# Adjusting contrast on one core: from phases of loads and stores on one DMA queue to half-size tiles on two queues

## The chip, the core and the metric

The kernel runs on one core of a Trainium2 chip. TensorE multiplies matrices, VectorE (DVE in the profile) and ScalarE (ACT) work on tiles in the on-chip memory SBUF, GpSimd (POOL) prepares constants, and SyncE (SP) issues DMA transfers. The data moves between the chip's HBM and SBUF through 16 DMA engines that belong to the core. The metric is the device time of the whole kernel in microseconds; lower is better.

## The reference

The input is 48 planes (16 images of 3 channels) of 512 x 512 float32. Every plane is pushed away from its own mean by a factor of 1.5 and clipped.

```python
def reference(x, factor):            # x: (16, 3, 512, 512) float32, factor 1.5
    mean = np.mean(x, axis=(2, 3), keepdims=True)
    return np.clip(mean + factor * (x - mean), 0, 1).astype(np.float32)
```

A plane has 1 MiB, so 50.33 MB are read and 50.33 MB are written. No pixel can be written before the whole plane has been read.

## The kernel before

The input is taken as one long row of numbers. A tile is 128 partitions with `ROW` = 16384 numbers (64 KB) each, 8 MiB in all, and contiguous in HBM; sixteen partitions hold one plane (`ppi`), a tile eight planes. There are six tiles, and a ring in SBUF with three slots (`BUFS` = 3); tile `t` lies in slot `t % BUFS` from its load to its store and is changed in place.

The steps of a tile, in `compute`:

- `add` sums each partition's row. VectorE reduces the first `SUM` = 4352 columns (line 85), ScalarE copies the rest onto itself with an accumulator (line 89). Tile 0 is summed in two halves, since it is loaded in pieces.
- TensorE (line 100) multiplies the sums with `blockw`, a matrix that is (1 − factor) / pixels within each block of sixteen partitions and zero elsewhere. The result, `shift`, is in every partition what must be added after the multiplication by the factor.
- VectorE runs over the row twice: multiply by the factor and add `shift` (line 103), then maximum with 0 and minimum with 1 (line 106).
- `store` (line 80) sends the row out. Tile 0 leaves in two pieces, cut at column `SHORT` = 2048.

The work is written out by hand in the order in which each engine does it: five loads for tiles 0 to 2, the computing and storing of tiles 0 to 2, the loads of tiles 3 to 5 (line 77), the computing and storing of tiles 3 to 5. Loads and stores are all issued by SyncE, so they stand in a single DMA queue in that order: three tiles in, three out, three in, three out. A load into a slot waits until the store that emptied it has finished. Synchronisation between the engines is derived from which tiles they read and write.

Of the kernel before, what the change touches and what calls it, by code (L numbers as in the profile page):

```python
# [1 line left out]

# [4 lines left out]


P = 128  # L10
ROW = 16384
HALF = ROW // 2
BUFS = 3
SHORT = 2048
SUM = 4352


@with_exitstack
def kernel(
    ctx: ExitStack,  # L20
    tc: tile.TileContext,
    x: bass.AP,
    factor: float,
    out: bass.AP,
):

    nc = tc.nc
    f32 = mybir.dt.float32  # L30
    Alu = mybir.AluOpType
    Act = mybir.ActivationFunctionType

    B, C, H, W = x.shape
    n_img, n_pix = B * C, H * W
    ppi = n_pix // ROW
    per_tile = P // ppi
    n_tiles = n_img // per_tile
    assert ppi * ROW == n_pix and per_tile * n_tiles == n_img

    factor = float(factor)
    wconst = (1.0 - factor) / float(n_pix)

    x_f = x.rearrange("b c h w -> (b c h w)")
    out_f = out.rearrange("b c h w -> (b c h w)")

    def dram(ap, t, c0=0, c1=ROW):
        return bass.AP(tensor=ap.tensor, offset=t * P * ROW + c0, ap=[[ROW, P], [1, c1 - c0]])

    consts = ctx.enter_context(tc.tile_pool(name="consts", bufs=1))  # L50
    xpool = ctx.enter_context(tc.tile_pool(name="xpool", bufs=1))
    small = ctx.enter_context(tc.tile_pool(name="small", bufs=1))
    psum = ctx.enter_context(tc.tile_pool(name="psum", bufs=1, space=bass.MemoryType.PSUM))


    sums = small.tile([P, 4 * n_tiles], f32, name="sums")
    bias = psum.tile([P, n_tiles], f32, name="bias")

    blockw = consts.tile([P, P], f32, name="blockw")
    blocks = blockw.rearrange("p (a b) -> p a b", b=ppi)  # L60
    nc.gpsimd.memset(blockw, wconst)  # L61
    for base, step in ((0, -ppi), (ppi - 1, ppi)):
        nc.gpsimd.affine_select(  # L63
            out=blocks,
            in_=blocks,
            compare_op=Alu.is_ge,
            fill=0.0,
            base=base,
            pattern=[[step, per_tile], [0, ppi]],
            channel_multiplier=1 if step < 0 else -1,  # L70
        )


    ring = xpool.tile([P, BUFS, ROW], f32, name="ring")

    def load(t, c0=0, c1=ROW):
        nc.sync.dma_start(out=ring[:, t % BUFS, c0:c1], in_=dram(x_f, t, c0, c1))  # L77

    def store(t, c0=0, c1=ROW):
        nc.sync.dma_start(out=dram(out_f, t, c0, c1), in_=ring[:, t % BUFS, c0:c1])  # L80

    def add(t, col, c0, c1, c2):
        xt = ring[:, t % BUFS, :]
        own = sums[:, 4 * t + col : 4 * t + col + 2]
        nc.vector.tensor_reduce(  # L85
            out=own[:, 0:1], in_=xt[:, c0:c1], axis=mybir.AxisListType.X, op=Alu.add
        )
        part = xt[:, c1:c2]
        nc.scalar.activation(out=part, in_=part, func=Act.Copy, accum_out=own[:, 1:2])  # L89
        return [own[:, 1:2], own[:, 0:1]]  # L90

    def compute(t, *cuts):
        xt = ring[:, t % BUFS, :]
        if t == 0:
            parts = add(t, 0, 0, SUM, HALF) + add(t, 2, HALF, HALF + SUM, ROW)
        else:
            parts = add(t, 0, 0, SUM, ROW)
        shift = bias[:, t : t + 1]
        for k, part in enumerate(parts):
            nc.tensor.matmul(shift, blockw, part, start=k == 0, stop=k == len(parts) - 1)  # L100
        for c0, c1 in zip((0, *cuts), (*cuts, ROW)):
            part = xt[:, c0:c1]
            nc.vector.tensor_scalar(  # L103
                out=part, in0=part, scalar1=factor, scalar2=shift, op0=Alu.mult, op1=Alu.add
            )
            nc.vector.tensor_scalar(  # L106
                out=part, in0=part, scalar1=0.0, scalar2=1.0, op0=Alu.max, op1=Alu.min
            )
            store(t, c0, c1)

    with tc.manual_schedule():
        load(0, 0, SHORT)
        load(0, SHORT, HALF)
        load(0, HALF, ROW)
        load(1)
        load(2)
        compute(0, SHORT)
        compute(1)
        compute(2)
        load(3)  # L120
        load(4)
        load(5)
        compute(3)
        compute(4)
        compute(5)


# [1 line left out]
_INS = ['x', 'factor']  # L129
_OUTS = [((16, 3, 512, 512), 'float32')]  # L130

_NUMBERS = {'factor': 1.5}


# [26 lines left out]
```

## Time and profile before

| | |
|---|---|
| time, median of 3 runs | 239.53 us (239.49 to 239.54) |
| span of the profiled execution | 237.3 us |
| HBM read / written | 50.33 MB / 50.33 MB |
| VectorE busy | 137.4 us (58%) |
| ScalarE busy | 59.9 us (25%) |
| TensorE matmul busy | 7.9 us (3%) |

The profiled execution has no time of its own beside its span; the timed runs lie 2.2 us above the span. In the rows, the first number is the start in microseconds from the span's start, or a busy time; PE is TensorE, SPq is the queue of SyncE's DMA issues; "L89" is line 89 of the kernel; the text behind an arrow "<-" in brackets names what ended the idle time before. In grouped rows, the numbers behind the bar are total busy microseconds, mean nanoseconds of one instruction, and idle time before it.

### The profile page before, as it was taken

How to read it: one execution, taken by the hardware profiler on the slowest of the kernel's cores; microseconds unless marked ns; L12 is line 12 of the kernel's file. 1: busy time of each engine (PE TensorE's matmuls, PEld its weight loads, DVE VectorE, ACT ScalarE, POOL GpSimd, SP SyncE). 2: the span in 40 equal slices, each digit the busy share in tenths (PEclk: the TensorE clock that was granted, in tenths of full speed). 3: DMA queues.
4: the chain of work that ended last, by engine and by line, in shares of the span. 5: the costliest groups of instructions: out<-in, count | busy, mean ns of one | idle time of the engine just before them, and what ended most of it. 6: DMA issues, size and time to landing. Idle time of an engine off the chain costs nothing.

```text
span 237.3 us, 186 instructions
## 1 busy us (share of the span) xinstructions
PE 7.9 (3%) x28; PEld 6.9 (3%) x28; DVE 137.4 (58%) x21; ACT 59.9 (25%) x15; POOL 1.1 (0%) x7
## 2 busy tenths in 40 slices
PE   0010100010001000000000000100000000000000
PEld 0010100010001000000000000100000000000000
DVE  0071899949998998000000043499989998991000
ACT  2051300980492000000000049319509800000000
POOL 1000000000000000000000000000000000000000
DMA  7999989899799798989899998989899998989894
GB/s 289 418 442 442 530 353 530 353 486 398 331 464 454 341 530 353 530 353 519 365 442 442 398 486 353 530 354 530 353 475 409 431 453 376 508 353 530 353 530 177
DMA packets 2160, 100.66 MB, mean 424 GB/s; under 512 B 240, under 2 KB 240, under 8 KB 240
## 3 DMA queue, kind: packets, MB, share of 16 engines
q1 hardware_dynamic: 2160, 100.66, 98.7%
HBM read 50.33 MB, written 50.33 MB: 424 GB/s over the span
## 4 chain that ended last, share of the span: by engine, by line
DVE 43%; DMA 36%; ACT 9%; PE 2%; SPq 1%; issue 0%; DVEq 0%; ACTq 0%
DMA ring<-in_x_dram 36%; DVE ring L103 18%; DVE ring L106 18%; ACT ring L89 9%; DVE sums L85 6%; PE bias L100 2%; SPq L77 1%; SPq L80 0%; DVEq L103 0%; ACTq L89 0%
## 5 line engine op out<-in xcount | busy, mean ns | idle before, releaser
L89 ACT ACTIVATE ring<-ring 128x12032 f32<-128x12032 f32 (+1 forms) x7 | 58.0, 8280 | 128.2 <-DMA ring<-in_x_dram 128.2
L85 DVE TENSOR_REDUCE sums<-ring 128x1 f32<-128x4352 f32 x7 | 32.8, 4683 | 63.9 <-DMA ring<-in_x_dram 63.9
L103 DVE TENSOR_SCALAR ring<-ring,bias 128x16384 f32<-128x16384 f32 (+2 forms) x7 | 52.8, 7538 | 12.9 <-PE bias L100 12.9
L106 DVE TENSOR_SCALAR ring<-ring 128x16384 f32<-128x16384 f32 (+2 forms) x7 | 52.3, 7476 | 0.2
L100 PE MATMUL bias<-sums,blockw 128*128 128x1 f32 x28 | 7.9, 360 | 189.1 <-ACT ring L89 175.4
L100 PEld LDWEIGHTS bias<-sums,blockw 128*128 128x128 f32 x28 | 6.9, 314 | 190.0 <-ACT ring L89 159.4
L89 ACT ACT_TABLE_LOAD x1 | 1.3, 1283 | 0.8 <-PEq L142 0.8
L89 ACT ACTIVATION_READ_ACCUMULATOR ring<-ring 128x1 f32 x7 | 1.3, 187 | 0.0
L63 POOL TENSOR_SCALAR_AFFINE_SELECT blockw<-blockw 128x128 f32<-128x128 f32 x2 | 0.7, 340 | 0.1
L61 POOL MEMSET blockw<- 128x128 f32 x1 | 0.2, 204 | 0.3 <-POOLq L142 0.3
L142 POOL MEMSET const-bfloat16-1.0<- 128x1 bf16 x1 | 0.1, 102 | 0.0
L142 POOL MEMSET const-uint8-127<- 128x1 uint8 x1 | 0.1, 102 | 0.0
L142 POOL MEMSET const-float32-0.0<- 128x1 f32 x1 | 0.1, 98 | 0.3 <-issue 0.3
L142 POOL MEMSET const-float32-1.0<- 128x1 f32 x1 | 0.1, 98 | 0.0
## 6 DMA issues: line engine op xcount, KB each, us to landing
out_dram<-ring SPq DMA_DIRECT2D x1, 7168.0 KB, 35.9
ring<-in_x_dram SPq DMA_DIRECT2D x1, 4096.0 KB, 20.8
ring<-in_x_dram SPq DMA_DIRECT2D x1, 3072.0 KB, 11.6
ring<-in_x_dram SPq DMA_DIRECT2D x1, 1024.0 KB, 4.7
out_dram<-ring SPq DMA_DIRECT2D x1, 1024.0 KB, 34.3
ring<-in_x_dram SPq DMA_DIRECT2D x5, 57.7
out_dram<-ring SPq DMA_DIRECT2D x5, 27.0
```

Of the source, the lines that this page charges most:

```text
L61: nc.gpsimd.memset(blockw, wconst)
L63: nc.gpsimd.affine_select(out=blocks, in_=blocks, compare_op=Alu.is_ge, fill=0.0, base=base, pattern=[[step, per_tile], [0, ppi]], channel ...
L77: nc.sync.dma_start(out=ring[:, t % BUFS, c0:c1], in_=dram(x_f, t, c0, c1))
L85: nc.vector.tensor_reduce(out=own[:, 0:1], in_=xt[:, c0:c1], axis=mybir.AxisListType.X, op=Alu.add)
L89: nc.scalar.activation(out=part, in_=part, func=Act.Copy, accum_out=own[:, 1:2])
L100: nc.tensor.matmul(shift, blockw, part, start=k == 0, stop=k == len(parts) - 1)
L103: nc.vector.tensor_scalar(out=part, in0=part, scalar1=factor, scalar2=shift, op0=Alu.mult, op1=Alu.add)
L106: nc.vector.tensor_scalar(out=part, in0=part, scalar1=0.0, scalar2=1.0, op0=Alu.max, op1=Alu.min)
L142: nc = _bacc.Bacc("TRN2", target_bir_lowering=False, num_devices=1)
```

## The change

Tiles have half the row, 8192 numbers (32 KB, 4 MiB a tile), so there are twelve of them, in a ring of six slots that occupies the same memory. SyncE issues loads alone: tiles 0 and 1 each in one transfer, tiles 2 and 3 in one of 8 MiB, tiles 4 and 5 likewise, and then one tile at a time, each when its slot is free. Stores are issued by ScalarE, on its own DMA queue. The sums of all tiles but the first are made by ScalarE alone; in tile 0 VectorE still reduces 4352 of the 8192 columns. Tile 0 is clipped and stored in three pieces of 1024, 2048 and 5120 columns (4, 8 and 20 KB a row). The order is a software pipeline: while VectorE clips tile `t`, ScalarE sums tile `t + 1`; for tiles 1 and 3 the store is issued ahead of that sum, for the others after it. The load of tile `t + 5` is issued after tile `t` in the program's order, and waits for the store of tile `t − 1`.

```diff
-ROW = 16384
-HALF = ROW // 2
-BUFS = 3
-SHORT = 2048
-SUM = 4352
+ROW = 8192
+BUFS = 6
+FIRST = (1024, 3072)
...
+    def load(t, n=1):
+        nc.sync.dma_start(out=slots(t, n), in_=dram(x_f, t, n=n))
 
     def store(t, c0=0, c1=ROW):
-        nc.sync.dma_start(out=dram(out_f, t, c0, c1), in_=ring[:, t % BUFS, c0:c1])
+        nc.scalar.dma_start(out=dram(out_f, t, c0, c1), in_=slots(t, 1, c0, c1))
...
+    def add(t, c0=0):
+        own = sums[:, 2 * t : 2 * t + 2]
+        parts = []
+        if c0:
+            nc.vector.tensor_reduce(
+                out=own[:, 0:1], in_=slots(t, 1, 0, c0), axis=mybir.AxisListType.X, op=Alu.add
+            )
+            parts.append(own[:, 0:1])
+        part = slots(t, 1, c0)
         nc.scalar.activation(out=part, in_=part, func=Act.Copy, accum_out=own[:, 1:2])
+        parts.insert(0, own[:, 1:2])
         shift = bias[:, t : t + 1]
         for k, part in enumerate(parts):
             nc.tensor.matmul(shift, blockw, part, start=k == 0, stop=k == len(parts) - 1)
...
+    def clip(t, c0=0, c1=ROW):
+        part = slots(t, 1, c0, c1)
...
...
     with tc.manual_schedule():
-        load(0, 0, SHORT)
-        load(0, SHORT, HALF)
-        load(0, HALF, ROW)
+        load(0)
         load(1)
-        load(2)
-        compute(0, SHORT)
-        compute(1)
-        compute(2)
-        load(3)
-        load(4)
-        load(5)
-        compute(3)
-        compute(4)
-        compute(5)
+        load(2, 2)
+        load(4, 2)
+        add(0, 4352)
+        for c0, c1 in zip((0, *FIRST), (*FIRST, ROW)):
+            clip(0, c0, c1)
+            store(0, c0, c1)
+        add(1)
+        for t in range(1, n_tiles):
+            clip(t)
+            if t in (1, 3):
+                store(t)
+            if t + 1 < n_tiles:
+                add(t + 1)
+            if t not in (1, 3):
+                store(t)
+            if t + BUFS - 1 < n_tiles:
+                load(t + BUFS - 1)
```

More of the change, by code (lines that the diff above doesn't have):

```diff
@@ L45, with dram @@
     out_f = out.rearrange("b c h w -> (b c h w)")
-    def dram(ap, t, c0=0, c1=ROW):
-        return bass.AP(tensor=ap.tensor, offset=t * P * ROW + c0, ap=[[ROW, P], [1, c1 - c0]])
+    def dram(ap, t, c0=0, c1=ROW, n=1):
+        run = [[P * ROW, n]] if n > 1 else []
+        return bass.AP(
+            tensor=ap.tensor, offset=t * P * ROW + c0, ap=[[ROW, P], *run, [1, c1 - c0]]
+        )
     consts = ctx.enter_context(tc.tile_pool(name="consts", bufs=1))
@@ L53 @@
     psum = ctx.enter_context(tc.tile_pool(name="psum", bufs=1, space=bass.MemoryType.PSUM))
-    sums = small.tile([P, 4 * n_tiles], f32, name="sums")
+    sums = small.tile([P, 2 * n_tiles], f32, name="sums")
     bias = psum.tile([P, n_tiles], f32, name="bias")
@@ L74, with slots @@
     ring = xpool.tile([P, BUFS, ROW], f32, name="ring")
-    def load(t, c0=0, c1=ROW):
-        nc.sync.dma_start(out=ring[:, t % BUFS, c0:c1], in_=dram(x_f, t, c0, c1))
-    def store(t, c0=0, c1=ROW):
[L80 to L97, printed above, removed]
+    def slots(t, n=1, c0=0, c1=ROW):
+        k = t % BUFS
+        return ring[:, k, c0:c1] if n == 1 else ring[:, k : k + n, :]
+    def load(t, n=1):
+        nc.sync.dma_start(out=slots(t, n), in_=dram(x_f, t, n=n))
+    def store(t, c0=0, c1=ROW):
+        nc.scalar.dma_start(out=dram(out_f, t, c0, c1), in_=slots(t, 1, c0, c1))
[5 more added lines that the diff above has]
+                out=own[:, 0:1], in_=slots(t, 1, 0, c0), axis=mybir.AxisListType.X, op=Alu.add
+            )
+            parts.append(own[:, 0:1])
+        part = slots(t, 1, c0)
+        nc.scalar.activation(out=part, in_=part, func=Act.Copy, accum_out=own[:, 1:2])
+        parts.insert(0, own[:, 1:2])
         shift = bias[:, t : t + 1]
@@ L100, in compute @@
             nc.tensor.matmul(shift, blockw, part, start=k == 0, stop=k == len(parts) - 1)
[L101 to L109, printed above, removed]
+    def clip(t, c0=0, c1=ROW):
+        part = slots(t, 1, c0, c1)
+        nc.vector.tensor_scalar(
+            out=part,
+            in0=part,
+            scalar1=factor,
+            scalar2=bias[:, t : t + 1],
+            op0=Alu.mult,
+            op1=Alu.add,
+        )
+        nc.vector.tensor_scalar(
+            out=part, in0=part, scalar1=0.0, scalar2=1.0, op0=Alu.max, op1=Alu.min
+        )
     with tc.manual_schedule():
-        load(0, 0, SHORT)
-        load(0, SHORT, HALF)
-        load(0, HALF, ROW)
+        load(0)
         load(1)
-        load(2)
-        compute(0, SHORT)
-        compute(1)
-        compute(2)
-        load(3)
-        load(4)
-        load(5)
-        compute(3)
-        compute(4)
-        compute(5)
+        load(2, 2)
[15 more added lines that the diff above has]
+                load(t + BUFS - 1)
 _INS = ['x', 'factor']
```

## The prediction

> **What bounds the kernel now.** I read the page first: the shares of the engines, then the DMA queue, whose share is far above all others.
>
> ```profile
> span 237.3 us, 186 instructions
> ...
> PE 7.9 (3%) x28; PEld 6.9 (3%) x28; DVE 137.4 (58%) x21; ACT 59.9 (25%) x15; POOL 1.1 (0%) x7
> ...
> q1 hardware_dynamic: 2160, 100.66, 98.7%
> HBM read 50.33 MB, written 50.33 MB: 424 GB/s over the span
> ```
>
> One queue, q1, carries everything, and the 16 DMA engines are busy with its packets for 98.7% of the span; VectorE works 58% of it, ScalarE 25%. So the question is not which engine computes faster, but how long the DMA engines need for the same 100.66 MB, and whether they ever run dry. For that I took the timeline. Where an ACT row waits for DMA, its start marks the landing of a load.
>
> ```profile
> 0.80 2.50 SPq L77 DMA_DIRECT2D ring<-in_x_dram  x5
> 12.86 3.40 ACT L89 ACTIVATE ring<-ring 128x3840 f32<-128x3840 f32 x1 [10.78 <-DMA ring<-in_x_dram]
> 22.58 3.40 ACT L89 ACTIVATE ring<-ring 128x3840 f32<-128x3840 f32 x1 [6.22 <-DMA ring<-in_x_dram]
> 27.94 1.29 DVE L103 TENSOR_SCALAR ring<-ring,bias 128x2048 f32<-128x2048 f32 x1 [0.68 <-PE bias L100]
> 30.52 63.63 SPq L80 DMA_DIRECT2D out_dram<-ring  x4
> 41.93 10.23 ACT L89 ACTIVATE ring<-ring 128x12032 f32<-128x12032 f32 x1 [15.86 <-DMA ring<-in_x_dram]
> 62.40 10.23 ACT L89 ACTIVATE ring<-ring 128x12032 f32<-128x12032 f32 x1 [10.15 <-DMA ring<-in_x_dram]
> 159.21 10.23 ACT L89 ACTIVATE ring<-ring 128x12032 f32<-128x12032 f32 x1 [8.96 <-DMA ring<-in_x_dram]
> 178.57 10.23 ACT L89 ACTIVATE ring<-ring 128x12032 f32<-128x12032 f32 x1 [9.04 <-DMA ring<-in_x_dram]
> ```
>
> The first half tile (4 MiB) has landed at 12.86, the second at 22.58: 9.72 us for 4 MiB in rows of 32 KB. Tile 1 (8 MiB, rows of 64 KB) lands 41.93 − 22.58 = 19.35 us later, tile 2 takes 62.40 − 41.93 = 20.47 us. Tile 3 is read off the chain of waits, whose DMA piece ends where the tile lands, at 94.24 + 45.52 = 139.76 us:
>
> ```profile
> 94.24 45.52 DMA ring<-in_x_dram
> ```
>
> Between 62.40 and 139.76 lie three stores and one load of 8 MiB: 77.36 us, 19.34 each. Tile 4 then takes 19.45, tile 5 19.36, and from 178.57 to the end of the span are three stores, 58.73 us, that is 3 × 19.35 and 0.68 us of tail. Loads and stores cost the same, 19.35 us for 8 MiB (8.39 MB in that time is 434 GB/s), with a scatter of about 0.1 us, and the only transfer out of line is the load of tile 2: it is the last load ahead of the first store of the run, and 1.12 us too long. The other turns between loads and stores show nothing above the scatter: tile 5, again the last load ahead of a store, needs 0.01 us more than the 19.35.
>
> The queue of SP says why the engines are never without work:
>
> ```profile
> SPq L80 <- DVE ring L106: 181.8, 7, 47.8
> SPq L77 <- DMA out_dram<-ring: 25.6, 2, 19.3
> ```
>
> SP waits long for clipped tiles, but behind work already queued; with the loads of three tiles ahead of it, the first store, issued at 30.52, cannot move before 62 anyway.
>
> **The change, part by part.** *Bytes and rows.* The 50.33 MB in and out stay. Rows shrink from 64 KB to 32 KB, and tile 0 leaves in rows of 4, 8 and 20 KB. The row for 32 KB is the 9.72 us above, against 9.675 for half of 19.35: 0.045 us per 4 MiB, over 23 such units 1.0 us. That difference is within the scatter, so it is worth between 0 and 1.0 us; I take the middle, 0.5. The small rows touch one of 24 units and I put them within the same bound.
>
> *Start and tail.* The first load is again issued at 0.80; its 4 MiB land at 12.86 as now. The tail of 0.68 us after the last store stays. So with the DMA engines always busy the span is 12.86 + 23 × 9.675 + 0.68 = 236.1 us, or 12.86 + 23 × 9.72 + 0.68 = 237.1 us; the middle is 236.6. Against 237.3 this lacks the stall of 1.12 us at the first store: now the load queue has rows waiting at that moment, which an engine can move meanwhile. That cover may fail, since the stalled packet may hold the engine itself; then 1.12 us come back.
>
> *Do the DMA engines run dry?* Here the compute counts. The rows by shape:
>
> ```profile
> L89 ACT ACTIVATE ring<-ring 128x12032 f32<-128x12032 f32 x5 | 51.2, 10231 | 111.2 <-DMA ring<-in_x_dram 111.2
> L85 DVE TENSOR_REDUCE sums<-ring 128x1 f32<-128x4352 f32 x7 | 32.8, 4683 | 63.9 <-DMA ring<-in_x_dram 63.9
> L103 DVE TENSOR_SCALAR ring<-ring,bias 128x14336 f32<-128x14336 f32 x1 | 7.7, 7685 | 0.0
> L106 DVE TENSOR_SCALAR ring<-ring 128x14336 f32<-128x14336 f32 x1 | 7.6, 7627 | 0.0
> L89 ACT ACTIVATE ring<-ring 128x3840 f32<-128x3840 f32 x2 | 6.8, 3402 | 17.0 <-DMA ring<-in_x_dram 17.0
> L89 ACT ACTIVATION_READ_ACCUMULATOR ring<-ring 128x1 f32 x7 | 1.3, 187 | 0.0
> L103 DVE TENSOR_SCALAR ring<-ring,bias 128x2048 f32<-128x2048 f32 x1 | 1.3, 1292 | 0.7 <-PE bias L100 0.7
> L106 DVE TENSOR_SCALAR ring<-ring 128x2048 f32<-128x2048 f32 x1 | 1.2, 1227 | 0.0
> ```
>
> ScalarE's sum costs (10231 − 3402) / 8192 = 0.834 ns per column, so 8192 columns take 3.40 + 4352 × 0.000834 = 7.0 us, with the read of the accumulator 7.2. VectorE's two passes cost 0.52 ns per column each (7685 − 1292 over 12288, and likewise L106): 2.52 us for 2048 columns, so 8.9 us for 8192. Twelve tiles are 107 us of clipping and one reduction of 4.7 on VectorE, and 83 us of sums on ScalarE, whose new store issues come on top:
>
> ```profile
> L80 SPq DMA_DIRECT2D out_dram<-ring x7: 332/343/348, 30.5 to 214.6; - x7
> 75.56 0.60 PE bias L100 x2
> ```
>
> 14 issues of 0.34 us are 4.8 us on ScalarE. Neither engine is near 237 us; the 28 us of reductions taken off VectorE lie beside transfers and are worth nothing. What ScalarE's new waits delay: while it waits for a clip to issue a store, the sum of a later tile is queued behind it.
>
> The order by hand, with shared DMA engines giving each queue every second row: from 22.58 to 27.94 the last sums of tile 0 take 5.4 us today, so after a landing at 12.86 the first clip starts at 18.2. The piece of 1024 columns takes 1.5 us, so the first store is issued at about 20, the second 2.5 us later, the third 5.7 us after that, at 28. Then ScalarE sums tile 1. The pieces are 24 rows per DMA engine, each alternating with a 32 KB load row of 9.7 / 8 = 1.21 us: 24 × 1.21 + 9.7 = 39 us, so tile 0 is out at about 59, when 4.7 tiles have been loaded. Load 6, which waits on SP for that store, is released 20 us before loads 4 and 5 end. From then on one tile goes in and one out every 19.4 us. Loads end at 59 + 7.3 × 19.4 = 200 us, with 8.3 tiles out. Tile 11 then needs 7.2 + 0.6 (the matmul row above) + 8.9 = 16.7 us, to 217, while the stores up to tile 10 last 2.7 × 9.7 = 26 us, to 226. The cover is 9 us deep; were it gone, up to 16.7 us would show. In mid-run a clip is ready 17 us after its landing, and the store queue then still holds the tile before. So no wait ends last except the DMA engines' own work.
>
> *Loads and stores at once.* This is the term that decides. Today the engines move only loads, then only stores; there are four stretches. After the change each engine alternates between two queues, and HBM is read and written together, from 20 to 200 us: 24 + 7 × 8 = 80 turns from a load row to a store row, on every engine. No row shows such alternation. The nearest ones are the two turns from loads to stores: 1.12 us for the first, 0.01 us for the second. The first stands beside the first store of the whole run and is not repeated, so I take the second as the nearer; what it can't show is the scatter of 0.1 us. So a turn costs from 0.01 to 0.1 us, 0.8 to 8 us in all; I choose 0.03, about the geometric middle, 80 × 0.03 = 2.4 us. Below nothing is possible as well, if two queues hide each other's row overhead; the 32 KB rows bound that at 1.0 us.
>
> One rule speaks against this change beside those turns. The Trainium skill (DMA: Bandwidth & Descriptors, section Latency and other measured facts) calls 214 GB/s per direction the full rate of copies on the sync and scalar queues in 16 KiB tiles; taken as loads and stores at once this is 428 GB/s, and against the 434 of the rows above 180 us of mixing would cost an estimated 2.5 us. No trace here shows that mixed rate.
>
> **Sum.** 236.6 + 2.4 = 239.0 us of span. The timed runs of before have a median of 239.53 for a profiled span of 237.3, a difference of 2.2 that I keep: 241.2 us, 0.7% slower.
>
> **Rivals.** *Alternation is free and the stall goes* (the other side). The engines move rows of either queue back to back, the stall of 1.12 us is filled with load rows, and rows of 32 KB run like those of 64 KB: 236.1 + 2.2 = 238.3 us, 0.5% faster. For it: the second turn cost 0.01. Against it: 80 turns instead of two. It decides if a turn costs under 0.01 us, since 80 × 0.01 already gives back 0.8 of the 1.2 us. Chance 0.20.
>
> *The queues merely interleave.* The engines share the work, what the stall gives the shorter rows and a few nanoseconds per turn take back: 237.1 + 2.2 = 239.3, within 0.2%. Chance 0.15. The Trainium skill (same page, section Issuing engines are not separate DMA queues) has just that rule, that transfers from both engines end on the same 16 DMA engines and interleave; 98.7% busy on one queue agrees with it.
>
> *Every turn costs real time.* If reading and writing disturb each other at 0.1 us or more a turn, with the stall kept, the span is 237.1 + 1.1 + 8 = 246 and the time 248.4 us or more; the 1.12 us is for it, the 0.01 against. Chance 0.08.
>
> *The store queue runs dry at the end.* If stores are served ahead of loads, the last load lands late, and up to 16.7 us of tile 11's compute show: 236.6 + 16.7 + 2.2 = 255.5. Against it is the cover of 9 us. Chance 0.03.
>
> **How the numbers follow.** The forecast, a turn at between 0.01 and 0.1 us, has 0.54; it spans 240.0, from where it can be told from no change, to 236.6 + 8 + 2.2 = 246.8. What a measurement can tell from no change is 0.2%, 0.5 us. Slower is 0.54 + 0.08 + 0.03 = 0.65, same 0.15, faster 0.20. The range goes from 238.0, just under the first rival, to 247.5, leaving out the two bad cases and the fringe of the first.
>
> **What would show it.** In the profile of the changed kernel: two DMA queues of 50.3 MB each; DMA share again near 98 to 99%; the first store issued near 20 us; load 11 landing near 200 us and the last store issued near 217, ten us before the DMA engines have emptied the queue. The mixing price is read from stretches between 60 and 200 us: 434 GB/s is the first rival, 428 to 430 the forecast, under 420 the third. I would be wrong if the DMA share fell in mid-run or at the end (compute or a slot was late), or if the mixed stretch moved more than 434 GB/s.

## The result and the profile after

| kernel | median | runs | ratio to before, 95% interval |
|---|---|---|---|
| before | 239.47 us (239.11 to 239.82) | 16 | |
| changed | 239.02 us (238.72 to 239.36) | 16 | 0.998 [0.9972, 0.9987] |

The change makes the kernel 0.2% faster, 0.45 us, close to the limit of what could be told from no change, though the interval leaves out 1. The forecast was 241.2 us, slower: the sign is wrong. The measured time lies inside the stated range, between the rival in which the queues merely interleave (239.3) and the one in which alternation is free (238.3).

The page of the changed kernel, the lines that answer to those of before, and its row of DMA rates in 40 slices:

```profile
span 237.0 us, 211 instructions
...
PE 7.6 (3%) x26; PEld 6.5 (3%) x26; DVE 112.1 (47%) x29; ACT 82.9 (35%) x25; POOL 1.0 (0%) x7
...
GB/s 265 442 442 442 398 459 383 441 428 435 465 426 404 409 442 442 442 442 442 442 426 431 404 420 442 442 442 442 442 442 426 415 398 442 442 442 442 442 442 265
...
q1 hardware_dynamic: 1696, 50.33, 49.6%
q10 hardware_dynamic: 2016, 50.33, 49.2%
HBM read 50.33 MB, written 50.33 MB: 425 GB/s over the span
```

There are two queues of 50.33 MB, and together they are busy for 98.8% of the span. VectorE lost 25 us, ScalarE gained 23, and the span has moved by 0.3 us. Most slices are as high while both queues run as in the first ones, where there are only loads. The exact price of mixing is in the timeline:

```profile
13.11 3.40 ACT L96 ACTIVATE ring<-ring 128x3840 f32<-128x3840 f32 x1 [11.03 <-DMA ring<-in_x_dram]
20.00 8.52 ACTq L85 DMA_DIRECT2D out_dram<-ring  x3
97.05 7.03 ACT L96 ACTIVATE ring<-ring 128x8192 f32<-128x8192 f32 x1 [5.21 <-DMA ring<-in_x_dram]
116.42 7.03 ACT L96 ACTIVATE ring<-ring 128x8192 f32<-128x8192 f32 x1 [12.25 <-DMA ring<-in_x_dram]
135.77 7.03 ACT L96 ACTIVATE ring<-ring 128x8192 f32<-128x8192 f32 x1 [12.23 <-DMA ring<-in_x_dram]
193.87 7.03 ACT L96 ACTIVATE ring<-ring 128x8192 f32<-128x8192 f32 x1 [12.25 <-DMA ring<-in_x_dram]
210.65 0.34 ACTq L85 DMA_DIRECT2D out_dram<-ring  x1
```

From the landing of tile 6 (97.05) to that of tile 11 (193.87) are five tiles in and, at the same pace, five out: 96.82 us, 19.36 for 4 MiB each way. Loads alone and stores alone took 19.35 us for the same 8 MiB in the kernel before. Put in chains by their starts and ends, 1120 of the 1280 rows that the DMA engines moved in this stretch follow a row of the other queue, which makes seven turns from a load to a store per tile on every engine; and a row of 32 KB takes 1213 ns at the median in either queue, as it does in the kernel before. So reading and writing at once, with a change of queue at nearly every row, costs 0.01 us per tile, nothing that can be seen. The first store is issued at 20.00 and the last at 210.65, with the DMA engines busy to the end.

### The profile page after: what moved, and what is told of

It is laid out like the page before. It is cut to its first block, busy times and chain, and to the rows that moved or that the text cites. A ratio compares the mean times of both kernels' runs of the same rounds, so it can differ in the third digit from the quotient of the medians.

```text
span 237.0 us, 211 instructions
## 1 busy us (share of the span) xinstructions
PE 7.6 (3%) x26; PEld 6.5 (3%) x26; DVE 112.1 (47%) x29; ACT 82.9 (35%) x25; POOL 1.0 (0%) x7
## 3 DMA queue, kind: packets, MB, share of 16 engines
q1 hardware_dynamic: 1696, 50.33, 49.6%
q10 hardware_dynamic: 2016, 50.33, 49.2%
HBM read 50.33 MB, written 50.33 MB: 425 GB/s over the span
## 4 chain that ended last, share of the span: by engine, by line
DMA 39%; DVE 25%; another core or an unknown queue 11%; ACT 9%; issue 3%; PE 1%; ACTq 1%; SPq 0%
DMA out_dram<-ring 20%; DMA ring<-in_x_dram 18%; DVE ring L104 11%; DVE ring L112 11%; ACT ring L96 9%; DVE sums L91 2%; PE bias L100 1%; ACTq L85 1%; SPq L82 0%
## 5 line engine op out<-in xcount | busy, mean ns | idle before, releaser
L96 ACT ACTIVATE ring<-ring 128x8192 f32<-128x8192 f32 (+1 forms) x12 | 80.7, 6724 | 117.3 <-DMA ring<-in_x_dram 95.3
L104 DVE TENSOR_SCALAR ring<-ring,bias 128x8192 f32<-128x8192 f32 (+3 forms) x14 | 54.3, 3880 | 84.9 <-PE bias L100 84.9
L112 DVE TENSOR_SCALAR ring<-ring 128x8192 f32<-128x8192 f32 (+3 forms) x14 | 53.4, 3817 | 0.5
L91 DVE TENSOR_REDUCE sums<-ring 128x1 f32<-128x4352 f32 x1 | 4.7, 4685 | 13.1 <-DMA ring<-in_x_dram 13.1
L96 ACT ACTIVATION_READ_ACCUMULATOR ring<-ring 128x1 f32 x12 | 2.2, 186 | 0.0
```

The costliest lines, as they stand in the source:

```text
L91: nc.vector.tensor_reduce(out=own[:, 0:1], in_=slots(t, 1, 0, c0), axis=mybir.AxisListType.X, op=Alu.add)
L104: nc.vector.tensor_scalar(out=part, in0=part, scalar1=factor, scalar2=bias[:, t : t + 1], op0=Alu.mult, op1=Alu.add,)
L112: nc.vector.tensor_scalar(out=part, in0=part, scalar1=0.0, scalar2=1.0, op0=Alu.max, op1=Alu.min)
```

## The experiments

The sixteen runs above stand for the changed kernel; each experiment has its ratio to the kernel before, run beside it.

### Rows, phases and queues

**e1_phases_32k**: the twelve tiles, but in phases on one queue; tile 0 leaves in one piece.

```diff
-        nc.scalar.dma_start(out=dram(out_f, t, c0, c1), ...
+        nc.sync.dma_start(out=dram(out_f, t, c0, c1), ...
...
+        for t in range(6):
+            load(t)
...
+            if t == 5:
+                for u in range(6, n_tiles):
+                    load(u)
```

> The changed kernel's twelve tiles of 32 KB rows, but loads and stores all on SyncE's queue in the phases of the kernel before: six tiles in, six out, six in, six out. Theory (turns between a load row and a store row are free on the DMA engines; the gain of the change is the smaller stall at the first stores): the stall of about 1.1 us at the first store is back and the shorter rows cost 0 to 0.8 us, so 239.4 to 240.2 us. Rival (turns do cost, and the shorter rows pay for them): phases with short rows have the gain without the price, under 238.8 us.

Measured: 239.26 us, ratio 0.9996 [0.9987, 1.0004]. That is 0.1 us under the theory's range and well above the rival's. The stall of the first store is there, though smaller; these are the landings of tiles 3, 4 and 5, in the timeline of e1:

```profile
42.15 7.03 ACT L97 ACTIVATE ring<-ring 128x8192 f32<-128x8192 f32 x1 [2.59 <-DMA ring<-in_x_dram]
51.86 7.03 ACT L97 ACTIVATE ring<-ring 128x8192 f32<-128x8192 f32 x1 [2.59 <-DMA ring<-in_x_dram]
62.28 7.03 ACT L97 ACTIVATE ring<-ring 128x8192 f32<-128x8192 f32 x1 [3.29 <-DMA ring<-in_x_dram]
```

A tile lands every 9.71 us, the last one ahead of the first store 10.42 us after its forerunner: a stall of 0.71 us. Twelve tiles in phases are as fast as six; so short rows alone don't explain the gain.

**e2_before_two_queues**: the kernel before, stores issued by ScalarE.

```diff
-        nc.sync.dma_start(out=dram(out_f, t, c0, c1), ...
+        nc.scalar.dma_start(out=dram(out_f, t, c0, c1), ...
```

> The kernel before with one edit: its stores are issued by ScalarE. Turns of 64 KB rows, tiles of 8 MiB. Theory: turns are free, but with tiles of 8 MiB ScalarE sums and waits in series, about 29 us from a landing to its store; by hand the last tile lands near 195, the store ahead of it ends near 215 and its own store is ready near 224, so the DMA engines are idle for about 9 us before the last store: 246 to 250 us, the idle slices at the end alone. Rival (turns cost): the stretches between 50 and 190 us move less than 430 GB/s as well. Rival (mixing itself gains, tile size does not matter): 239 us or less.

Measured: 254.52 us, ratio 1.0637 [1.0604, 1.067]. The DMA row of its page shows where:

```profile
DMA  7999899898999799797998979999799997303977
```

Each slice is 6.28 us. The engines are full up to slice 34 and stand at 3, 0 and 3 tenths in the slices 35 to 37, 214 to 232 us. The mechanism was foreseen, its size not: 15 us of idle time instead of 9, since the last tile landed at 200.56 and not 195, and its store left at 229.63. The rival that turns cost finds no support: tiles 3 and 5 land at 122.91 and 200.56, two tiles in and two out in 77.65 us, 19.4 for 8 MiB. Two queues want small tiles: with 8 MiB a tile is 29 us from its landing to its store, more than the stores behind which it could hide.

**e3_after_one_queue**: the changed kernel, stores issued by SyncE.

```diff
-        nc.scalar.dma_start(out=dram(out_f, t, c0, c1), ...
+        nc.sync.dma_start(out=dram(out_f, t, c0, c1), ...
```

> The changed kernel with one edit: stores are issued by SyncE, on the loads' queue, so loads and stores alternate by whole tiles of 4 MiB and not by rows. Theory (free turns; only rows, start, tail and the first stall count): 239.0 to 239.8 us, the stall at the first store near 60 us back. Rival (two queues themselves gain, rows of one hide the gaps of the other): 0.5 to 1.5 us above the changed kernel in steady stretches, 239.5 to 240.5, spread over the run. Rival (SyncE's waits for clipped tiles hold loads back): idle slices in the middle.

Measured: 242.29 us, ratio 1.0108 [1.0089, 1.0128]; 3.3 us over the changed kernel. The theory's range is missed; the first rival has the direction, but with 0.5 to 1.5 us less than half of the size. The one queue is busy 97.9% of a longer span, so the engines stand idle for 5.1 us on average, against 2.8 in the changed kernel. There is no idle slice in the middle; the last slice of its DMA row has 2 tenths where the changed kernel has 6:

```profile
span 240.6 us, 210 instructions
...
DMA  7999999999899999999999999999999999999992
...
q1 hardware_dynamic: 3712, 100.66, 97.9%
```

The landings are late one by one:

```profile
91.91 7.03 ACT L96 ACTIVATE ring<-ring 128x8192 f32<-128x8192 f32 x1 [15.45 <-issue]
111.64 7.03 ACT L96 ACTIVATE ring<-ring 128x8192 f32<-128x8192 f32 x1 [12.62 <-DMA ring<-in_x_dram]
131.72 7.03 ACT L96 ACTIVATE ring<-ring 128x8192 f32<-128x8192 f32 x1 [12.95 <-DMA ring<-in_x_dram]
191.33 7.03 ACT L96 ACTIVATE ring<-ring 128x8192 f32<-128x8192 f32 x1 [12.42 <-DMA ring<-in_x_dram]
```

Five tiles take 99.42 us, 19.88 each and not 19.36. It would be easy to call the half microsecond the price of the one turn from a load to a store per tile, but the trace speaks against that. A tile has landed when the slowest of the 16 DMA engines is done, and the trace has the end of each. For tile 6 the ends lie between 90.8 and 91.8 us, for tile 11 between 187.7 and 191.3: the first ends and the middle ones are 19.4 us a tile apart, and only the last are 19.9, though every engine makes the same turns. At the end of the run ten engines are done by 236.7, five between 237.7 and 238.4, and the last at 239.8; in the changed kernel all end between 235.8 and 236.2. In the windows view of e3, the last stretch has one row of 32 KB on one engine (13 GB/s over 2.5 us):

```profile
237.00:239.50 2.50, 0.00 (x0) 0.00 (x0) 0.00 (x0) 0.00 (x0) 0.00 (x0) 1.00 0.03 13
```

So what e3 loses is for the most part that a few engines fall behind the others; why they do is not shown. In this order a second queue is worth more than the time of issuing. The Trainium skill (DMA: Bandwidth & Descriptors, section Issuing engines are not separate DMA queues) says that a second issuing engine saves only the sequencer's time; here it saved 3.3 us at equal tiles, and the measurement decides. It is not so for every order: in phases, one queue (e1) was only 0.24 us behind the changed kernel.

**e4_before_no_cut**: the kernel before with `compute(0)` in place of `compute(0, SHORT)`.

> The kernel before with tile 0 stored in one piece of 64 KB rows. It asks what the 1.1 us at the first store is. If it is the first write to HBM of the run: it stays, 239.4 us, tile 2 still lands 20.4 us after tile 1. If it is the turn into the small rows of 8 KB: tile 2 lands 19.4 us after tile 1 and the time is 238.3 to 238.6 us.

Measured: 239.58 us, ratio 1.0007 [0.9998, 1.0015]. Tile 1 lands at 41.95, tile 2 at 62.58, 20.63 us later; the stall stays, so the small rows are not its cause.

### Many more turns

**e6_mixed_8k_rows** and **e7_phases_8k_rows**: every transfer cut into four by columns, in the changed kernel (tile 0 without its pieces) and in e1.

```diff
+PIECE = 2048
...
+            for c in range(0, ROW, PIECE):
+                nc.sync.dma_start(out=slots(u, 1, c, c + PIECE), in_=dram(x_f, u, c, c + PIECE))
...
```

> The changed kernel with every load and store in four transfers of rows of 8 KB (tile 0 stored in the same rows): four times as many turns between a load row and a store row on each DMA engine, some 300. To be held against the same rows in phases on one queue (e7_phases_8k_rows), which has two turns. Theory (turns between two queues are free): shorter rows and more completions cost 2 to 4 us, 241 to 243 us, and this kernel is no slower than the one in phases. Rival (a turn costs 0.01 to 0.03 us): 2.4 to 7 us above the kernel in phases.

> The twelve tiles in phases on SyncE's one queue (as e1_phases_32k), with every transfer cut into four with rows of 8 KB. Both theories: 241 to 243.5 us, rows and completions alone; it is the reference for e6_mixed_8k_rows.

Measured: e6 242.62 us, ratio 1.013 [1.0116, 1.0144]; e7 243.99 us, ratio 1.0187 [1.0173, 1.0201] and 0.5 us over what was expected. Chains of its rows, made as above, give about 160 turns per engine in e6 against 66 in the changed kernel: 2.4 times as many and not four, since a queue often moved several small rows in a row. With them the mixed kernel is 1.4 us faster than the one in phases; the rival put it 2.4 to 7 us behind. No price per turn between two queues can be seen here either.

### ScalarE adds

**e8_after_vector_adds**: `add(t, 4352)` for every tile.

> The changed kernel with VectorE reducing 4352 of the 8192 columns of every tile, as it does in tile 0. VectorE gets some 52 us more work, ScalarE 40 us less. Theory (compute is under cover): 238.8 to 239.3 us, as the changed kernel. Rival (taking the reductions off VectorE is part of the gain): 239.5 us or more.

Measured: 239.23 us, ratio 0.9992 [0.9982, 1.0003], within the theory's range. Who sums is not a visible part of the gain: at 0.2 us over the changed kernel, the intervals of the two ratios overlap.

### The pieces of tile 0

**e5_after_no_pieces**: `FIRST = ()`.

> The changed kernel with tile 0 stored in one piece of 32 KB rows: the first store leaves at 28 us and not at 20. Theory (the DMA engines are never dry, so it does not matter when the first store leaves): 238.8 to 239.3 us, as the changed kernel. Rival (the small first pieces soften the stall at the first store): the stall of about 1 us is back and the time is 239.5 to 240 us.

Measured: 242.56 us, ratio 1.0134 [1.0115, 1.0153]. Both are wrong; the loss is three times a single stall. Three landings in the timeline, and from the timeline of SP the issue of a load that waits for a store to end:

```profile
110.77 7.03 ACT L96 ACTIVATE ring<-ring 128x8192 f32<-128x8192 f32 x1 [5.74 <-DMA ring<-in_x_dram]
131.13 7.03 ACT L96 ACTIVATE ring<-ring 128x8192 f32<-128x8192 f32 x1 [13.24 <-DMA ring<-in_x_dram]
210.53 7.03 ACT L96 ACTIVATE ring<-ring 128x8192 f32<-128x8192 f32 x1 [12.63 <-DMA ring<-in_x_dram]
```

```profile
133.81 20.38 SPq L82 DMA_DIRECT2D ring<-in_x_dram  x2
```

Five tiles take 99.76 us, 19.95 each. And a store ends (133.81) 2.7 us after a load has landed (131.13): loads and stores come to the ends of their tiles together. In the changed kernel the same tile lands at 116.42, and the next store ends at 123.66, 7.2 us later:

```profile
123.66 0.33 SPq L82 DMA_DIRECT2D ring<-in_x_dram  x1
```

The new theory was that being in step costs. Seven kernels with other first stores were to tell it from the rivals, that small rows, an early store, or a divided store of tile 0 is what helps.

**e9_pieces_late**: the stores of the three pieces in reverse, `reversed(...)`, after the last clip. **e10_two_halves**: `FIRST = (4096,)`. **e11_five_eighths**: `FIRST = (5120,)`. **e12_halves_late**: as e10, with both clips written ahead of both stores. **e13_whole_later**: `FIRST = ()` and `add(1, 4352)` ahead of `clip(0)`. **e14_halves_last_first**: as e10, with the stores in reverse. **e15_whole_at_32**: `FIRST = ()`, and `add(1, 4352)` between the two passes of `clip(0)`.

> The changed kernel with its three pieces of tile 0, but all three stored after the last clip, so the first store leaves at 28 us and not at 20, with the largest piece first. A store of tile 0 is still 24 rows per DMA engine, three tiles' worth of load rows. Theory (what costs is that loads and stores reach the ends of their tiles together: a store that starts near 30.6 us starts where load 3 does, after 24 rows, and stays in step): 241.5 to 243 us, tiles land 19.6 to 20.1 us apart from 100 us on, as without pieces. Rival (small first rows are what helps): 238.8 to 239.4 us, tiles 19.35 us apart.

> The changed kernel with tile 0 stored in two halves of 16 KB rows, no small rows. The first half leaves near 23 us and starts about two rows into a load's eight. Theory (out of step is what helps): 238.8 to 239.4 us, tiles 19.35 us apart. Rival (small first rows are what helps): 241 to 243 us.

> The changed kernel with tile 0 stored in a piece of 20 KB and one of 12 KB rows. The first leaves near 24.2 us and starts about four rows into a load's eight, the farthest from being in step. Theory (out of step is what helps): 238.8 to 239.4 us, tiles 19.35 us apart. Rival (a late first store costs, whatever the step): 240 to 242 us, between the changed kernel and the one without pieces.

> The kernel of e10_two_halves with both halves stored after the last clip, at 28 us: 16 rows of 16 KB for tile 0, starting near 30.6 us where load 3 starts, and done near 60 us, before the load queue is empty, so loads and stores stay in step. Theory (being in step is what costs): 241.5 to 243 us, tiles 19.6 to 20.1 us apart from 100 us on, as without pieces. Rival (one undivided store of tile 0 is what costs): 238.8 to 239.5 us.

> The changed kernel with tile 0 stored whole, as without pieces, but later: VectorE reduces 4352 columns of tile 1 ahead of the clip of tile 0, which moves the first store from 28 to about 36 us, some six rows further, two rows short of the next step. Theory (being in step is what costs): 238.8 to 239.6 us, tiles 19.35 us apart from 100 us on. Rival (one undivided or late store of tile 0 is what costs): 242 us or more.

> Tile 0 stored in two halves of 16 KB rows, the second half first, so that the first store waits for the last clip and leaves at 28 us, where the whole-tile store left: a divided store that starts where load 3 starts, 16 rows long, so loads and stores are in step. Theory (being in step costs): 241 to 243 us, tiles up to 20 us apart. Rival (the undivided store of tile 0 costs): 238.8 to 239.5 us, tiles 19.35 us apart.

> Tile 0 stored whole, with VectorE's reduction of 4352 columns of tile 1 between the two passes over tile 0: the store leaves at about 32 us and starts four rows into a load's eight, as far from being in step as can be; e13 came out eight rows later than without pieces, at 37 us, and so in step again. Theory (being in step costs): 238.8 to 239.5 us, tiles 19.35 us apart. Rival (the undivided store of tile 0 costs): 240.8 to 242.6 us.

Measured. The first store is ScalarE's first issue; the lag is from the landing of tile 7 to the next end of a store, read like the rows above; the spacing is the mean of five tiles from tile 6 to 11. Under "engines end" stand the first and the last of the 16 DMA engines to finish the last store. These columns are read from one profiled execution, whose own time stands beside the median.

| kernel | first store | tile 0 | lag | spacing | engines end | profiled | median | ratio to before |
|---|---|---|---|---|---|---|---|---|
| changed | 20.0 us | three pieces | 7.2 | 19.36 | 235.8 to 236.2 | 238.72 us | 239.02 us | 0.998 [0.9972, 0.9987] |
| e9 | 28.3 | three pieces | 11.2 | 19.36 | 236.0 to 236.6 | 239.12 | 239.50 | 1.0 [0.9988, 1.0013] |
| e10 | 23.2 | halves | 13.1 | 19.35 | 236.0 to 236.5 | 239.07 | 238.98 | 0.9975 [0.9966, 0.9984] |
| e12 | 23.2 | halves | 13.3 | 19.35 | 235.9 to 236.3 | 238.95 | 238.93 | 0.9981 [0.9972, 0.999] |
| e11 | 24.6 | 20 and 12 KB | 16.3 | 19.35 | 236.0 to 237.0 | 239.57 | 239.19 | 0.9985 [0.9975, 0.9995] |
| e15 | 32.0 | whole | 8.2 | 19.37 | 236.2 to 237.0 | 239.63 | 239.28 | 0.999 [0.9981, 0.9999] |
| e8 | 19.9 | three pieces | 5.8 | 19.45 | 236.0 to 236.8 | 239.44 | 239.23 | 0.9992 [0.9982, 1.0003] |
| e14 | 27.8 | halves | 2.0 | 19.46 | 235.9 to 238.0 | 240.56 | 239.99 | 1.0013 [0.9998, 1.0029] |
| e13 | 37.2 | whole | 1.6 | 19.47 | 236.1 to 238.3 | 240.94 | 240.96 | 1.0068 [1.0054, 1.0081] |
| e5 | 27.6 | whole | 2.7 | 19.95 | 238.3 to 240.7 | 243.41 | 242.56 | 1.0134 [1.0115, 1.0153] |

Three of these runs were not what they were meant to be. e9 was to be in step and fell out of it: tile 0 left only at 72 us, the load that waits for it came late to its queue, and the loads went on from a new place. e12 changed nothing, since every engine works off its own list and the order in which VectorE's and ScalarE's instructions are written against each other does not matter: its first half left at 23.2 us as in e10, and it is a repeat of that. e13 was to be out of step and came out a whole eight rows later, in step again.

Taken as what they are, the ten kernels part by their lag. With a lag of 7 us or more the spacing is 19.35 to 19.37, with pieces or without, with the first store at 20 us or at 32 us (e15, an undivided store, the opposite of e5). With a lag under 3 us it is 19.46 to 19.95, with a divided store too (e14). e8, between them with 5.8 us, has 19.45. So neither small rows, nor an early nor a divided store, is what helps, and the loss goes with a store that ends soon after a landing.

That this is its cause is not shown. No run set the lag directly, and the size does not follow it: e14, expected at 241 to 243, took 239.99, with runs from 238.91 to 240.56, while e5 has a longer lag and loses most. It isn't nearness as such either: a store ends every 19.4 us, so in e11, with a lag of 16.3, one ends 3 us ahead of each landing, and that costs nothing. The ends of the engines say more. In e13 and e14 the first engines are done as early as in the kernels that lose nothing, and the time is lost by the last few, as in e3, where there is only one queue; in e5 all are late, the first by 2.5 us. e9 stands apart: its profiled execution, the quickest of its twelve, has the narrow spacing, and its median shows no gain over the kernel before. What makes engines fall behind is open.

## Why the prediction was wrong

What holds: the DMA engines are the bound before and after, at 98.7% and 98.8%. The base of 236.1 to 237.1 us of span held in the profiled execution (237.0), and so did the compute: 7.03 us for a sum, 20.0 us for the first store. Loads ended at 193.87 us, a little ahead of the 200 expected, and the last store was issued at 210.65 and not 217, 26 us ahead of the end of the span; less its own 9.7 us and the tail, its cover was about 16 us and not 9. The 28 us of reductions taken off VectorE were worth nothing (e8).

The step that failed is the term "loads and stores at once", 80 turns at 0.03 us or 2.4 us. It was placed between a stall seen once and a scatter, with nothing to say that rows alternating between two queues pay what a turn within one queue pays. The runs show that they don't: 19.36 against 19.35 us for 8 MiB, and with rows of 8 KB a mixed kernel with 160 turns ahead of the one in phases. (The count was high too: about 66 turns and not 80.) The reading of 428 GB/s from the Trainium skill's copies pointed the same wrong way: 8.39 MB in 19.36 us is 433 GB/s with both directions at once. Without the term the sum is 236.6 + 2.2 = 238.8, against 239.02. That it comes so near is in part luck. The profiled execution does have a time of its own, 238.72 us for a span of 237.0, and the timed runs of both kernels lie 1.7 to 1.8 us above their own spans; the 2.2 held a median against the span of one quick execution. The median time of the changed kernel belongs to a span of about 237.3, so the base is 0.7 us too low and the addition 0.5 too high.

The first rival had the sign right and over a third of its 1.2 us. The stall of 1.12 us was meant to vanish. With the measured pace the span after would be 13.11 + 23 × 9.68 + 0.68 = 236.4 us; it is 237.0. The 0.6 us are lost outside the stretch from 97 to 194 us and may be half of the stall, still paid. In phases with the same rows (e1) there is no gain that can be told from none, 239.26, so the 0.45 us come for the most part from the second queue with its order, not from the smaller tiles. The split of 0.45 us between the lost stall, the rows and the evenness of the engines is under what these runs resolve.

That it does not matter when the first store leaves, which the schedule by hand implied, was right for the time and wrong for the place: the first store also sets how loads and stores lie against each other for the rest of the run, and a bad place went with a loss of up to 3.5 us, eight times the whole effect of the change.

## What to carry to other kernels

When the DMA engines are busy 98% of the span, the bytes set the time, and an order of work can only lose against that; ask what the change could make worse, and price only what a row supports. Two queues that carry loads and stores at once ran at the full rate here, provided that tiles are small enough for a store to be ready while others are still leaving (e2), and that a store didn't end just after a load had landed (e5); the distance is quickly read off the timeline. A landing is that of the slowest of 16 DMA engines: a tile that lands late does not mean that all of them were slow, and the last slice of the DMA row shows when a few end after the rest. An edit that shifts one transfer shifts all that alternate with it, so a difference that seems to belong to the edit may belong to the step: try a second shift before believing it.

## What the runs showed of the hardware that was not expected

Between two queues that alternated by rows of 32 KB, a tile in and a tile out cost 0.01 us more than without alternation. Within one queue the first turn from loads to stores of a run cost 0.7 to 1.3 us whatever the rows of the store were (0.71 in e1, 1.12 before, 20.63 − 19.35 = 1.28 in e4). The 16 DMA engines of one run did not keep together: with loads and stores by turns in one queue (e3) the ends of one transfer came to lie 3.6 us apart, with the middle engine at 19.4 us a tile and the last at 19.9, and in e13 and e14 the last store's ends lie 2.1 to 2.2 us apart, against 0.4 in the changed kernel.
